# Conditioning pieces of the head: more places to load into, other moments for the loads, longer bursts

## The chip, the cores and the metric

The kernel runs on one core of a Trainium2 chip. The metric is the device time of one execution in microseconds. Three timed runs of the kernel before gave 1992.62, 1993.09 and 1994.77 us; their median is 1993.09 us. One more execution was profiled.

## The reference, cut to what matters

A decoder layer is run for 256 prompt tokens and 8 times 8 sample tokens (320 columns in all, width 2048). Only the first step matters here:

```python
mod = jax.nn.silu(c) @ w_ada + b_ada                      # (.., 6 * 2048), c: one row per sequence
sh1, sc1, g1, sh2, sc2, g2 = jnp.split(mod, 6, axis=-1)
h = _rmsnorm(x, norm1_g) * (1 + sc1) + sh1
p = h @ w_in                                              # 11280 columns
```

Before any row tile of h exists, its part of sh1 and sc1 must be there, which needs all 2048 rows of two column ranges of w_ada (2048 x 12288, float32). Everything after h (linear attention, pooling, w_o, the FFN) is the same in both kernels.

## The kernel before, in words

The part around the change is called the head. h is kept transposed, as 16 row tiles of 128 x 320, each split into a high and a low part (`hh`, `hl`). The 16 tiles are worked off in five slices, `SLICES` = 0-2, 2-4, 4-8, 8-12, 12-16. In each slice 15 units of 256 columns of w_in (the q, k, v, u, og, ga and gb columns of group 0, and the gb columns of groups 1 and 3) are multiplied by the tiles of that slice, and each unit's result is added in SBUF. A tile costs a unit two halves of three matmuls of 320 columns (lines 166 to 168), so a unit of a two-tile slice has 12 matmuls and a unit of a four-tile slice 24. In the two-tile slices the units v, og, ga and the three gb come in pairs that share one load (`proj_pair`); q, k and u are single.

While slice n is multiplied, `HeadJob` works out the conditioning (sh1, sc1) of the tiles of slice n+1: it loads w_ada in pieces of 512 KB (`load`), multiplies them on TensorE in bursts (`burst`, `ada_mm`, line 218; four column groups side by side, a float32 matmul shows as two instructions), then transposes the sums and adds the bias (`finish`), and `h_unit(k)` makes tile k of h from it. These steps stand in a list `bg`, and `after_unit` takes a share of them after each of the 15 units, so step i of a list of 15 runs after unit i. For a slice of two tiles there are four bursts, each of 32 instructions of 128 columns; for a slice of four tiles there are eight, each of 16 instructions of 256 columns.

Every load of w_ada and w_in is issued by one queue, SP's (line 142), and `keep_in_program_order` holds them there in the order in which the program calls them. A load waits on SP until its place in SBUF is free, and all loads behind it wait too. w_in has three places of 512 KB (`raw`), w_ada eight of 512 KB (`araw`). Each `burst` calls for the pieces of itself and of the next two bursts. When a piece of w_in has landed, ACT casts it to its high part (line 152), DVE makes the low part (line 153), and the matmuls start. Before the slices, x's rows stand in three tiles `xn0` to `xn2` of 128 x 2048; they are transposed into `xT` and then not read again; `junk`, of the same size, holds c's rows and the discarded squares. The slice-0 job has all eight `araw` places filled at the start. `spill` writes `xT` to DRAM through POOL's queue.

Of the kernel before, what the change touches and what calls it, by code (L numbers as in the profile page):

```python
# [11 lines left out]
F32 = mybir.dt.float32  # L12
# [8 lines left out]
P = 128  # L21
# [3 lines left out]
D = 2048  # L25
KT = D // P
# [12 lines left out]
SLICES = ((0, 2), (2, 4), (4, 8), (8, 12), (12, 16))  # L39
# [41 lines left out]
def body(tc, A):  # L81
# [15 lines left out]
    def nm(s):  # L97
        uid[0] += 1
        return "%s_%d" % (s, uid[0])

    def misc():
        return pmisc.tile([P, 512], F32, tag="m", name=nm("pm"))
# [32 lines left out]
    def raw_chunk(src, nk, nn, pool=None, tag="raw", bufs=3):  # L135

        if pool is None and more:
            more.reverse()
            if more[0] is not None:
                pool, bufs = more[0], 2  # L140
        t = (pool or wp).tile([P, nk, nn], F32, tag=tag, bufs=bufs, name=nm("raw"))
        ins = nc.sync.dma_start(t, src)
        if in_order[0]:
            tc.keep_in_program_order(ins)
        return t
# [63 lines left out]
    wada = A["w_ada"][0].rearrange("(kt p) n -> p kt n", p=P)  # L209
# [5 lines left out]
    def ada_mm(ps, k, raws, w, start=None, stop=None):  # L215

        for j in range(4):
            ins = PE.matmul(ps[32 * j:32 * j + 32, 0:w], lhsT=scT[:, k, :], rhs=raws[j],  # L218
                            start=k == 0 if start is None else start, stop=k == KT - 1 if stop is None else stop,
                            tile_position=(0, 32 * j))  # L220
            if j == 0:
                tc.keep_in_program_order(ins)

    def ada_out(dst, src, blk, shape):

        n = dst.shape[1]
        sec = blk // KT

        def wide(v):
            return v.rearrange("p (m c) -> p m c", m=shape[0]).unsqueeze(3).broadcast_to([P, *shape, 9])  # L230

        d4 = dst.rearrange("p (m c) r -> p m c r", m=shape[0])
        V.tensor_tensor(d4, src, wide(bada[:, blk:blk + n]), op=ALU.add)
        if sec in (1, 4):
            b0 = blk - sec * KT
            V.tensor_tensor(d4, d4, wide((N1G if sec == 1 else N2G)[:, b0:b0 + n]), op=ALU.mult)
# [53 lines left out]
    def modp(sec, kt):  # L290
        return mod[:, sec * KT + kt, 0:1]

    def mods(sec, kt):
        return mod[:, sec * KT + kt, 1:9].unsqueeze(2).broadcast_to([P, NB, LS])

    def s3(ap):
        return ap.rearrange("p (b t) -> p b t", t=LS)
# [79 lines left out]


    with tc.tile_pool(name="head", bufs=1) as xp:
        junk = xp.tile([P, D], F32, name="junk")  # L380
        crow = junk[0:9, :]
        nc.sync.dma_start(crow[0:1, :], A["c_prompt"])
        nc.sync.dma_start(crow[1:9, :], A["c_sample"])
        xn = [xp.tile([P, D], F32, name="xn%d" % i) for i in range(3)]
        x2d = A["x_prompt"][0]
        nc.sync.dma_start(xn[0], x2d[0:P])
        nc.sync.dma_start(xn[1], x2d[P:2 * P])
# [18 lines left out]
        def pinned(ins):  # L406
            tc.keep_in_program_order(ins)

        class HeadJob:


            def __init__(self, b0, s):
                self.b0, self.s, self.w, self.nk = b0, s, 64 * s, 8 // s
                self.ps = None
                self.raws = {}

            def load(self, k0):
                if k0 >= KT or k0 in self.raws:
                    return
                c = self.b0 * P  # L420
                self.raws[k0] = [raw_chunk(wada[:, k0:k0 + self.nk, sec * D + c:sec * D + c + self.s * P], self.nk,
                                  self.s * P, xp, "araw", 8) for sec in range(2)]

            def burst(self, k0):
                for ahead in range(3):
                    self.load(k0 + ahead * self.nk)
                raws = self.raws[k0]
                self.raws[k0] = None
                if self.ps is None:
                    self.ps = misc()  # L430
                w = self.w
                for i in range(self.nk):
                    ada_mm(self.ps, k0 + i, [raws[j // 2][:, i, (j % 2) * w:(j % 2) * w + w] for j in range(4)], w)

            def finish(self):
                nb = self.s // 2
# [6 lines left out]
                for sec in range(2):  # L443
                    blk = sec * KT + self.b0
                    ada_out(mod[:, blk:blk + self.s, :], src[:, 2 * sec:2 * sec + 2, :, 0:9], blk, (2, nb))

            def steps(self):
                return ([lambda: self.load(0)] + [lambda k0=k0: self.burst(k0) for k0 in range(0, KT, self.nk)]
                        + [self.finish])


        xT = []
        for k in range(KT):
            pt = misc()
            for i in range(3):
                n = P if i < 2 else TS
# [17 lines left out]
        for i in range(3):  # L474
            n = P if i < 2 else TS
# [5 lines left out]
        for i in range(3):  # L481
            n = P if i < 2 else TS
# [5 lines left out]
        def h_unit(k):  # L488
            t = xp.tile([P, T], F32, tag="xh", bufs=2, name=nm("xh"))
            V.scalar_tensor_tensor(t[:, 0:TP], xT[k][:, 0:TP], modp(1, k), rx[:, 0:TP], op0=ALU.mult, op1=ALU.mult)  # L490
            G.tensor_tensor(t[:, TP:T], xT[k][:, TP:T], rx[:, TP:T], op=ALU.mult)
            G.tensor_tensor(s3(t[:, TP:T]), s3(t[:, TP:T]), mods(1, k), op=ALU.mult)
            G.tensor_tensor(s3(t[:, TP:T]), s3(t[:, TP:T]), mods(0, k), op=ALU.add)
            S.activation(hh[k][:, 0:TP], t[:, 0:TP], AF.Identity, bias=modp(0, k))
            S.copy(hh[k][:, TP:T], t[:, TP:T])
            hl[k] = hp.tile([P, T], F32R, tag="hl%d" % k, name="hl%d" % k)
            V.scalar_tensor_tensor(hl[k][:, 0:TP], t[:, 0:TP], modp(0, k), hh[k][:, 0:TP].bitcast(F32),
                                   op0=ALU.add, op1=ALU.subtract)
            V.tensor_sub(hl[k][:, TP:T], t[:, TP:T], hh[k][:, TP:T].bitcast(F32))  # L499

        def spill(k0, k1):
            for k in range(k0, k1):
                pinned(nc.gpsimd.dma_start(xspill[k], xT[k]))
# [21 lines left out]
        for h in EARLY_GB:  # L525
            ge = G0()
            ge.gb = merged[h]
            early += [(ge, "gb", i, OGB + DV * h + 256 * i) for i in range(2)]
        for f in HeadJob(0, SLICES[0][1]).steps():
            f()  # L530
        for k in range(SLICES[0][1]):
            h_unit(k)
        for si, (k0, k1) in enumerate(SLICES):
            bg = []
            acc = 0 if si == 0 else 1
            if si + 1 < len(SLICES):
                n0, n1 = SLICES[si + 1]
                if si == 0:
                    bg.append(lambda: spill(0, SLICES[1][1]))
                else:  # L540
                    bg.append(lambda n0=n0, n1=n1: spill(n0, n1))
                bg += HeadJob(n0, n1 - n0).steps()
                bg += [lambda k=k: h_unit(k) for k in range(n0, n1)]
            if si == len(SLICES) - 2:
                walr = xp.tile([P, KT, 16], F32, name="walr")
                cum = xp.tile([P, NM0 + NM1 + NMS], F32, name="cum")

                def late_loads():
                    pinned(nc.gpsimd.dma_start(walr, win[:, :, OAL:OAL + 16]))
                    pinned(nc.gpsimd.dma_start(msk, A["ci"]))  # L550
                    pinned(nc.gpsimd.dma_start(cum, A["cf"][:, 64:CFW]))
                    pinned(nc.gpsimd.dma_start(invc, A["cf"][:, 0:64]))
                bg.insert(1, late_loads)
            def after_unit():
                count[1] += 1
                if si == len(SLICES) - 1 and count[1] == 2:
                    alr_proj(walr, cum)
                want = len(bg) * count[1] // len(early)
                while count[0] < want:
                    bg[count[0]]()  # L560
                    count[0] += 1

            count = [0, 0]
            e = 0
            while e < len(early):
                ge, kind, i, col = early[e]
                if k1 - k0 == 2 and kind not in "qku":
                    for half, ps in enumerate(proj_pair(win, col, k0, k1, hh, hl)):
                        evac(ps, ge, kind, half, acc)
                        after_unit()  # L570
                    e += 2
                else:
                    evac(proj(win, col, k0, k1, hh, hl), ge, kind, i, acc)
                    after_unit()
                    e += 1
# [436 lines left out]
    for ui in range(8):  # L1012
# [4 lines left out]
        for i in range(2):  # L1017
            residual(ps, i, 2 * ui + i, 2)
            k = 2 * ui + i
# [35 lines left out]
    for pi, (f0, f1) in enumerate(parts):  # L1055
# [22 lines left out]
        for ui in range(8):  # L1078
            ps = proj(wdn, 256 * ui, f0, f1, ah, al)
            for i in range(2):  # L1080
                k = 2 * ui + i
                residual(ps, i, k, 5)
                if pi == 1:
# [4 lines left out]
                    for a in range(3):  # L1088
                        n = P if a < 2 else TS
                        tr(pt[:n, a * P:(a + 1) * P], xg[:, a * P:a * P + n])  # L1090
                    for a in range(3):
                        n = P if a < 2 else TS
# [6 lines left out]
    for a in range(3):  # L1099
        n = P if a < 2 else TS  # L1100
        PE.matmul(pt[:n, 2 * a:2 * a + 2], lhsT=acc2[:, a * P:a * P + n], rhs=ones[:, 0:2], start=True, stop=True)
    rr = fp.tile([P, 64], F32, name="rr")[:, 0:6]
    for a in range(3):
        n = P if a < 2 else TS
# [3 lines left out]
    for a in range(3):  # L1108
        n = P if a < 2 else TS
# [30 lines left out]
```

## Time and profile before

| what | value |
|---|---|
| timed runs, median | 1993.09 us |
| profiled execution, its own time | 1993.81 us |
| span of the profile (first to last instruction) | 1992.0 us |
| PE busy | 1942.7 us, 98% |
| DVE, ACT, POOL busy | 51%, 41%, 7% |
| DMA, mean over the span | 201 GB/s |
| granted TensorE clock, mean | 0.991 |

The profiled execution's time is its span and 1.8 us around it. A busy share of an engine is that of the time in which an instruction of it was running. DMA share is the busy share of the core's 16 DMA engines; it can read a little above 1 where packets overlap.

### The profile page before, as it was taken

The numbers are of one execution on the slowest core, as the hardware profiler recorded it, in microseconds if no ns is written. First come the engines' busy times: TensorE is split into PE (matmuls) and PEld (weight loads), VectorE is DVE, ScalarE is ACT, GpSimd is POOL, SyncE is SP. The second block draws the span as 40 slices with busy tenths as digits, with TensorE's granted clock in tenths as the row PEclk, the third lists the DMA queues.
The fourth block names the chain that finished last, engine by engine and source line by source line (L and its number), as shares of the span: only waits on it lengthen the run. The fifth ranks groups of instructions, "written<-read, shape, count | busy, mean of one in ns | idle before, by whom it ended". The sixth has DMA issues, their size and how long they took to land.

```text
span 1992.0 us, 37175 instructions
## 1 busy us (share of the span) xinstructions
PE 1942.7 (98%) x15008; PEld 1848.6 (93%) x15008; DVE 1014.1 (51%) x1881; ACT 819.6 (41%) x1468; POOL 137.5 (7%) x261
## 2 busy tenths in 40 slices
PE   7999999999999999999989999999999999999997
PEld 5789998898999899889979999999999999999997
DVE  2556665574546544664574444344444444444554
ACT  4333374364335333643353333343333434344443
POOL 1112220111011100110030000000000000000000
PEclk9999999999999999999989999999999999999998
DMA  9888754775975787579636666544445544444442
GB/s 296 287 303 271 230 165 147 263 262 187 325 245 174 269 266 234 167 248 339 226 112 223 202 221 193 167 150 143 156 147 151 153 152 148 149 148 149 148 143 90
DMA packets 319598, 400.83 MB, mean 201 GB/s; under 512 B 13529, under 2 KB 259801, under 8 KB 319089
## 3 DMA queue, kind: packets, MB, share of 16 engines
q1 hardware_dynamic: 307154, 358.21, 56.1%
q0 software_dynamic: 12272, 40.25, 5.4%
q8 instruction: 117, 1.92, 0.4%
q14 instruction: 55, 0.45, 0.1%
HBM read 373.96 MB, written 24.67 MB: 200 GB/s over the span
## 4 chain that ended last, share of the span: by engine, by line
PE 93%; DMA 4%; DVE 1%; ACT 1%; issue 1%; SPq 0%; POOL 0%; ACTq 0%; POOLq 0%; DVEq 0%
PE ps L166 27%; PE ps L168 27%; PE ps L167 27%; PE pm L218 5%; PE pm L129 2%; DMA raw<-w_ada 1%; DMA raw<-w_in 1%; DMA raw<-w_o 1%; PE pm L804 1%; PE pm L825 1%; PE pm L773 1%; DMA xn<-x_sample 1%; PE pm L800 0%; PE pm L762 0%; DVE wlo L153 0%
## 5 line engine op out<-in xcount | busy, mean ns | idle before, releaser
L153 DVE TENSOR_TENSOR wlo<-raw,whi 128x512 fp32r<-128x512 f32 x952 | 658.6, 696 | 817.5 <-ACT whi L152 807.5
L152 ACT CAST whi<-raw 128x512 fp32r<-128x512 f32 x952 | 586.3, 621 | 995.4 <-PE ps L167 843.8
L166 PE MATMUL ps<-hh,whi 128*128 128x320 f32 x1408 | 443.3, 315 | 6.5 <-ACT whi L152 3.0
L166 PE MATMUL ps<-h2h,whi 128*128 128x320 f32 x1408 | 437.4, 311 | 5.1 <-ACT h2h L1046 5.1
L168 PE MATMUL ps<-hh,wlo 128*128 128x320 f32 x1408 | 440.4, 313 | 0.1
L167 PE MATMUL ps<-hl,whi 128*128 128x320 f32 x1408 | 438.7, 312 | 0.4 <-DVE hl L499 0.4
L168 PE MATMUL ps<-h2h,wlo 128*128 128x320 f32 x1408 | 435.5, 309 | 0.0
L167 PE MATMUL ps<-h2l,whi 128*128 128x320 f32 x1408 | 435.5, 309 | 0.0
L166 PEld LDWEIGHTS ps<-hh,whi 128*128 128x128 f32 x1408 | 265.6, 189 | 25.6 <-issue 11.8
L168 PEld LDWEIGHTS ps<-hh,wlo 128*128 128x128 f32 x1408 | 265.6, 189 | 7.9 <-issue 5.7
L166 PEld LDWEIGHTS ps<-h2h,whi 128*128 128x128 f32 x1408 | 265.0, 188 | 8.5 <-ACT h2h L1046 6.1
L167 PEld LDWEIGHTS ps<-hl,whi 128*128 128x128 f32 x1408 | 265.7, 189 | 7.5 <-issue 5.9
L167 PEld LDWEIGHTS ps<-h2l,whi 128*128 128x128 f32 x1408 | 264.9, 188 | 0.0
L168 PEld LDWEIGHTS ps<-h2h,wlo 128*128 128x128 f32 x1408 | 264.9, 188 | 0.0
L166 PE MATMUL ps<-ah,whi 128*128 128x320 f32 x704 | 218.7, 311 | 0.0
L168 PE MATMUL ps<-ah,wlo 128*128 128x320 f32 x704 | 217.5, 309 | 0.0
L167 PE MATMUL ps<-al,whi 128*128 128x320 f32 x704 | 217.5, 309 | 0.0
L167 PEld LDWEIGHTS ps<-al,whi 128*128 128x128 f32 x704 | 132.2, 188 | 0.0
L166 PEld LDWEIGHTS ps<-ah,whi 128*128 128x128 f32 x704 | 132.2, 188 | 0.0
L168 PEld LDWEIGHTS ps<-ah,wlo 128*128 128x128 f32 x704 | 132.2, 188 | 0.0
L218 PE MATMUL pm<-raw,scT 128*32 128x128 f32 (+1 forms) x2688 | 104.7, 296 | 4.3 <-DMA raw<-w_ada 4.3
L218 PEld LDWEIGHTS pm<-raw,scT 128*32 128x32 f32 x2688 | 72.0, 112 | 25.3 <-issue 13.6
(279 smaller groups left out, 1538.2 us busy)
## 6 DMA issues: line engine op xcount, KB each, us to landing
raw<-w_ada SPq DMA_DIRECT2D x192, 512.0 KB, 6.1
raw<-w_gu SPq DMA_DIRECT2D x176, 512.0 KB, 3.5
raw<-w_in SPq DMA_DIRECT2D x173, 512.0 KB, 4.3
raw<-w_down SPq DMA_DIRECT2D x80, 512.0 KB, 3.4
S<-state_gla POOLq DMA_DIRECT2D x16, 1024.0 KB, 8.7
o_gs<-S POOLq DMA_DIRECT2D x16, 1024.0 KB, 7.6
raw<-w_o SPq DMA_DIRECT2D x32, 512.0 KB, 5.3
raw<-w_down SPq DMA_DIRECT2D x16, 256.0 KB, 2.5
```

Of the source, the lines that this page charges most:

```text
L129: PE.transpose(out, in_, ident[:k, :k])
L152: S.copy(hi, raw)
L153: V.tensor_sub(lo, raw, hi.bitcast(F32))
L166: PE.matmul(ps, lhsT=whi, rhs=xhi, start=start, stop=False)
L167: PE.matmul(ps, lhsT=whi, rhs=xlo, start=False, stop=False)
L168: PE.matmul(ps, lhsT=wlo, rhs=xhi, start=False, stop=stop)
L218: ins = PE.matmul(ps[32 * j:32 * j + 32, 0:w], lhsT=scT[:, k, :], rhs=raws[j], start=k == 0 if start is None else start, stop=k == KT - 1 ...
L773: PE.matmul(pt, lhsT=E["kdn"][:, s, d * P:(d + 1) * P], rhs=E["vn"][:, s], start=s == 0, stop=s == 1)
L804: PE.matmul(pt[32 * j:32 * j + 32, :], lhsT=qeP[:, d, 4 * gg + j, :], rhs=E["S0", gg, d][:, j], start=False, stop=d == 1, tile_position=(0 ...
L825: PE.matmul(pt, lhsT=kpz[:, gg, j, d * P:(d + 1) * P], rhs=E["vp"][:, gg], start=True, stop=True)
```

## The change

Three things change in `HeadJob` and in the lists that call it.

- w_ada pieces get four more places of 1 MB each: the tiles `xn0`, `xn1`, `xn2` and `junk`, once x's rows are done with. Pieces of 1 MB go there, pieces of 512 KB to `araw` as before.
- The bursts are longer. The slice of two tiles behind slice 0 has two bursts of eight row tiles (64 instructions of 128 columns); a slice of four tiles has four bursts of four row tiles (32 instructions of 256 columns). Slice 0's own job keeps four bursts of 32 instructions.
- The loads are steps of their own. In slice 0 all 4 MB of slice 1's job are called for after units 1 and 2, and the four bursts' pieces of slice 2's job (2 MB each) after units 8, 11, 14 and 15. In slice 1 and 2 the pieces of the job two slices on follow after units 5, 8, 12 and 15. Bursts come after units 7 and 10 in slice 0, and after units 2, 4, 7 and 9 later (in the fourth slice one step list is longer by one).

```diff
@@ class HeadJob
-            def load(self, k0):
-                if k0 >= KT or k0 in self.raws:
-                    return
+                if b0 == 0:
+                    self.bursts = [[(k, 4)] for k in range(0, KT, 4)]
+                elif s == 2:
+                    self.bursts = [[(0, 8)], [(8, 8)]]
+                else:
+                    self.bursts = [[(0, 2), (2, 2)], [(4, 2), (6, 2)], [(8, 4)], [(12, 4)]]
+            def load(self, b):
                 c = self.b0 * P
-                self.raws[k0] = [raw_chunk(wada[:, k0:k0 + self.nk, sec * D + c:sec * D + c + self.s * P], self.nk,
-                                  self.s * P, xp, "araw", 8) for sec in range(2)]
+                for k, n in self.bursts[b]:
+                    for sec in range(2):
+                        src = wada[:, k:k + n, sec * D + c:sec * D + c + self.s * P]
+                        if n * self.s == 8:
+                            r = raw_chunk(src, n, self.s * P, xp, "araw", 8)
+                        else:
+                            r = raw_chunk(src, n, self.s * P, xp, BIG[2 * (b % 2) + sec], 1)
+                        self.raws[k, sec] = r
-            def burst(self, k0):
-                for ahead in range(3):
-                    self.load(k0 + ahead * self.nk)
...
+            def burst(self, b):
...
+                todo = [(k, i) for k, n in reversed(self.bursts[b]) for i in range(n)]
+                for k, i in todo:
+                    ada_mm(self.ps, k + i, ...)
...
@@ the lists
-        for f in HeadJob(0, SLICES[0][1]).steps():
-            f()
+        jobs = [HeadJob(k0, k1 - k0) for k0, k1 in SLICES]
+        for b in range(4):
+            jobs[0].load(b)
+        for b in range(4):
+            jobs[0].burst(b)
+        jobs[0].finish()
...
                 if si == 0:
-                    bg.append(lambda: spill(0, SLICES[1][1]))
+                    bg += [load(job, 0), load(job, 1), sp, rest, rest, rest, burst(0), load(nxt, 0), rest, burst(1),
+                           load(nxt, 1), job.finish, hu[0], load(nxt, 2), hu[1], load(nxt, 3)]
                 else:
-                    bg.append(lambda n0=n0, n1=n1: spill(n0, n1))
-                bg += HeadJob(n0, n1 - n0).steps()
-                bg += [lambda k=k: h_unit(k) for k in range(n0, n1)]
+                    bg += [sp, burst(0), rest, burst(1), load(nxt, 0), rest, burst(2), load(nxt, 1), burst(3),
+                           job.finish, hu[0], load(nxt, 2), *hu[1:], load(nxt, 3)]
```

`BIG` is ("xn0", "xn1", "xn2", "junk"), `job` the job of the next slice, `nxt` that of the slice after it, `rest` an empty step, `sp` the spill, `hu` the h_units.

## Rows read from the trace of the kernel before

**Rows 1.** Stretches of 25 us: length, busy of each engine, clock, DMA share, GB/s

```profile
25.00:50.00 25.00, 21.29 (x243) 19.07 (x243) 9.22 (x24) 8.72 (x18) 5.57 (x11) 0.93 0.87 293
...
75.00:100.00 25.00, 21.95 (x204) 16.27 (x196) 12.24 (x20) 6.42 (x11) 0.00 (x0) 1.00 0.89 315
...
150.00:175.00 25.00, 25.00 (x190) 23.72 (x180) 18.59 (x36) 10.77 (x22) 10.09 (x20) 1.00 0.66 198
```

**Rows 2.** Timeline of PE in slice 1: start, duration, instruction, idle before and releaser

```profile
83.17 0.41 PE L166 MATMUL ps<-hh,whi 128*128 128x320 f32 x1 [1.41 <-ACT whi L152]
...
90.92 0.41 PE L166 MATMUL ps<-hh,whi 128*128 128x320 f32 x1 [1.63 <-ACT whi L152]
...
109.84 0.39 PE L166 MATMUL ps<-hh,whi 128*128 128x320 f32 x1 [0.33 <-DVE hl L499]
```

**Rows 3.** Timeline of SP's queue, ahead of the first of these waits

```profile
75.87 0.88 SPq L142 DMA_DIRECT2D raw<-w_ada  x2
76.85 0.42 SPq L142 DMA_DIRECT2D raw<-w_in  x1
```

**Rows 4.** Timeline of PE around three bursts, of 32, 16 and 48 instructions

```profile
51.30 0.31 PE L167 MATMUL ps<-hl,whi 128*128 128x320 f32 x1
51.45 0.31 PE L168 MATMUL ps<-hh,wlo 128*128 128x320 f32 x1
51.69 1.08 PE L218 MATMUL pm<-raw,scT 128*32 128x128 f32 x32
52.70 0.41 PE L166 MATMUL ps<-hh,whi 128*128 128x320 f32 x1
52.95 0.31 PE L167 MATMUL ps<-hl,whi 128*128 128x320 f32 x1
...
125.79 1.07 PE L218 MATMUL pm<-raw,scT 128*32 128x256 f32 x16
...
315.31 1.52 PE L218 MATMUL pm<-raw,scT 128*32 128x128 f32 x48
316.76 0.40 PE L644 MATMUL pm<-cumr,w 128*128 128x272 f32 x1
```

**Rows 5.** Instructions by line on PE, 35.00 to 69.39 us (slice 0)

```profile
L166 PE MATMUL ps<-hh,whi 128*128 128x320 f32 x60 | 19.6, 329 | 2.9 <-ACT hh L495 2.7 <-DVE v L355 0.2
```

**Rows 6.** Timeline of PE: the last transposes of x's rows

```profile
23.17 1.63 PE L129 MATMUL pm<-cst,xn 128*128 128x128 f32 x5
```

**Rows 7.** Stretches in which the DMA engines were full, columns as in rows 1

```profile
14.00:24.00 10.00, 10.00 (x34) 5.06 (x34) 3.37 (x11) 5.08 (x11) 0.00 (x0) 1.00 1.10 349
...
29.50:45.50 16.00, 12.46 (x131) 11.21 (x124) 6.43 (x18) 5.34 (x11) 5.25 (x10) 0.89 1.00 330
...
79.00:94.00 15.00, 11.95 (x104) 9.20 (x103) 5.80 (x10) 2.28 (x4) 0.00 (x0) 1.00 1.02 373
...
99.00:119.00 20.00, 19.45 (x137) 17.84 (x137) 16.65 (x33) 8.60 (x18) 7.46 (x16) 1.00 1.01 365
```

**Rows 8.** DMA issues of the first 300 us: count, size, median us to landing

```profile
raw<-w_ada SPq DMA_DIRECT2D x67, 512.0 KB, 6.4
```

**Rows 9.** The loads of w_ada and w_in as one tile, first 300 us

```profile
DMA to landing us min/median/max: 2.8/5.8/13.1
```

**Rows 10.** Timeline of ACT: a cast that waited for its load

```profile
90.25 1.14 ACT L152 CAST whi<-raw 128x512 fp32r<-128x512 f32 x2 [6.61 <-DMA raw<-w_in]
```

**Rows 11.** Timeline of PE at the start of slice 0

```profile
35.33 0.56 PE L166 MATMUL ps<-hh,whi 128*128 128x320 f32 x2 [2.67 <-ACT hh L495]
...
38.58 0.47 PE L166 MATMUL ps<-hh,whi 128*128 128x320 f32 x1
38.85 0.47 PE L167 MATMUL ps<-hl,whi 128*128 128x320 f32 x1
```

**Rows 12.** A stretch inside it, columns as in rows 1

```profile
38.00:39.40 1.40, 1.40 (x7) 1.40 (x7) 0.00 (x0) 0.00 (x0) 0.65 (x2) 0.50 1.03 312
```

**Rows 13.** GB/s of the first 300 us in 40 equal slices

```profile
GB/s 242 281 348 206 307 365 286 185 260 360 346 344 317 261 399 335 188 302 327 242 210 107 225 337 393 320 316 336 205 192 143 140 325 377 193 142 95 101 141 114
```

More of the change, by code (lines that the diff above doesn't have):

```diff
@@ L379, in body @@
     with tc.tile_pool(name="head", bufs=1) as xp:
-        junk = xp.tile([P, D], F32, name="junk")
+        BIG = ("xn0", "xn1", "xn2", "junk")
+        junk = xp.tile([P, D], F32, tag="junk", name="junk")
         crow = junk[0:9, :]
@@ L383, in body @@
         nc.sync.dma_start(crow[1:9, :], A["c_sample"])
-        xn = [xp.tile([P, D], F32, name="xn%d" % i) for i in range(3)]
+        xn = [xp.tile([P, D], F32, tag="xn%d" % i, name="xn%d" % i) for i in range(3)]
         x2d = A["x_prompt"][0]
@@ L412, in __init__ @@
             def __init__(self, b0, s):
-                self.b0, self.s, self.w, self.nk = b0, s, 64 * s, 8 // s
+                self.b0, self.s, self.w = b0, s, 64 * s
                 self.ps = None
                 self.raws = {}
-            def load(self, k0):
-                if k0 >= KT or k0 in self.raws:
-                    return
-                c = self.b0 * P
-                self.raws[k0] = [raw_chunk(wada[:, k0:k0 + self.nk, sec * D + c:sec * D + c + self.s * P], self.nk,
-                                  self.s * P, xp, "araw", 8) for sec in range(2)]
-            def burst(self, k0):
-                for ahead in range(3):
-                    self.load(k0 + ahead * self.nk)
-                raws = self.raws[k0]
-                self.raws[k0] = None
+                if b0 == 0:
[5 more added lines that the diff above has]
+            def load(self, b):
+                c = self.b0 * P
+                for k, n in self.bursts[b]:
[7 more added lines that the diff above has]
+            def burst(self, b):
                 if self.ps is None:
@@ L431, in burst @@
                 w = self.w
-                for i in range(self.nk):
-                    ada_mm(self.ps, k0 + i, [raws[j // 2][:, i, (j % 2) * w:(j % 2) * w + w] for j in range(4)], w)
+                todo = [(k, i) for k, n in reversed(self.bursts[b]) for i in range(n)]
+                for k, i in todo:
+                    ada_mm(self.ps, k + i,
+                           [self.raws[k, j // 2][:, i, (j % 2) * w:(j % 2) * w + w] for j in range(4)], w,
+                           b == 0 and (k, i) == todo[0], b == len(self.bursts) - 1 and (k, i) == todo[-1])
             def finish(self):
@@ L445, in finish @@
                     ada_out(mod[:, blk:blk + self.s, :], src[:, 2 * sec:2 * sec + 2, :, 0:9], blk, (2, nb))
-            def steps(self):
-                return ([lambda: self.load(0)] + [lambda k0=k0: self.burst(k0) for k0 in range(0, KT, self.nk)]
-                        + [self.finish])
         xT = []
@@ L537, in body, with load, burst, rest @@
                 n0, n1 = SLICES[si + 1]
+                job = jobs[si + 1]
+                nxt = jobs[si + 2] if si + 2 < len(SLICES) else None
+                def load(j, b):
+                    return (lambda: j.load(b)) if j else (lambda: None)
+                def burst(b):
+                    return lambda: job.burst(b)
+                def rest():
+                    return None
+                hu = [lambda k=k: h_unit(k) for k in range(n0, n1)]
+                sp = lambda n0=n0 if si else 0, n1=n1: spill(n0, n1)
                 if si == 0:
-                    bg.append(lambda: spill(0, SLICES[1][1]))
-                else:
-                    bg.append(lambda n0=n0, n1=n1: spill(n0, n1))
-                bg += HeadJob(n0, n1 - n0).steps()
-                bg += [lambda k=k: h_unit(k) for k in range(n0, n1)]
+                    bg += [load(job, 0), load(job, 1), sp, rest, rest, rest, burst(0), load(nxt, 0), rest, burst(1),
+                           load(nxt, 1), job.finish, hu[0], load(nxt, 2), hu[1], load(nxt, 3)]
+                else:
+                    bg += [sp, burst(0), rest, burst(1), load(nxt, 0), rest, burst(2), load(nxt, 1), burst(3),
+                           job.finish, hu[0], load(nxt, 2), *hu[1:], load(nxt, 3)]
             if si == len(SLICES) - 2:
```

## Prediction

> **What bounds the kernel now.** Over the whole span PE is busy 98% of the time, so a change can win only where PE idles or where it does needless work. I read first the stretches of 25 us, because the change touches only the head (about the first 240 us). There PE is short of work twice: 3.7 us between 25 and 50, and 3.0 us between 75 and 100; by 150 to 175 it has no idle time while DMA is at two thirds [rows 1]. Second, the timeline of PE says what ended those gaps. The first is the wait for the first tile of h, before slice 0, which the change leaves alone. The second is two waits in slice 1, 1.41 and 1.63 us, both ended by ACT's cast of a w_in piece [rows 2]. Third, SP's queue says why that cast was late: the w_in load went out at 76.85, directly behind two w_ada pieces that had waited at 75.87 for a burst to free their places [rows 3]. So PE bounds the head from slice 2 on, and in slices 0 and 1 it runs close to what the DMA queue delivers: DMA is 0.87 to 0.89 busy there [rows 1].
>
> **The bursts.** Matmuls of the main stream start 0.147 us apart (51.30 to 51.45 shows 0.15). Around a burst of 32 instructions the starts run 51.45, 51.69, 52.70, 52.95: 1.50 us where two steps would be 0.29, so the burst costs 1.21 us. A burst of 48 runs 1.45 us from its start to the next matmul against 1.01, so 16 more instructions of 128 columns cost 0.44, and of the 1.21 us some 0.33 are entry and exit. Sixteen instructions of 256 columns take 1.07 against 1.08, the same [rows 4]. A burst of the new size is 64 instructions of 128 columns or as much: 1.21 + 2 x 0.44 = 2.09 us. The job run in slice 0 had four bursts (4.84) and gets two (4.18): 0.66 saved. Each of the three four-tile jobs had eight (9.68, or 9.6 with the 256-column rows) and gets four (8.36): 1.2 saved each. Together 4.3 us, all on PE and so on the path. No row shows a burst of this length: it can't cost more than two of 32 (2.42, nothing saved), nor less than its instructions without any entry (1.76, some 9 saved over the 14 bursts); the step from 32 to 48 is the nearest row, so I take 2.09. The two waits of slice 1 are worth 3.0 more if nothing replaces them.
>
> **The loads.** Here I add up what SP's queue must move in program order. A w_ada piece is 512 KB, 0.524 MB [rows 8]; a 1 MB piece is two of them. A single unit of a two-tile slice loads 0.262 MB, a pair 0.524. Ahead of the first w_in load of slice 1 now stand all of slice 1's job (8 x 0.524 = 4.19 MB), all of slice 2's job (8.39 MB; before only slice 1's job stood there), slice 0's w_in (3.93 MB), four spills of 0.164 MB on the other queue (0.66), and the load itself (0.26): 17.4 MB.
>
> When does this start? The first two pieces go into xn0 and xn1, whose last transposes end at 23.17 + 1.63 = 24.8 [rows 6]. The quickest landing of all was 2.8 us, for a load whose bytes take some 0.8 of it, so about 2.0 us are fixed [rows 9]; the queue flows from 26.8. How fast? Stretches with the engines full gave 349 and 330 GB/s early on, where the loads are 256 columns wide, and 373 and 365 later, where most are 512 wide [rows 7]. I take 340 and 370, near the middle of each pair. 5.24 MB are of the narrow kind (slice 1's job, q, k, u, and q again): 15.4 us. 12.19 MB of the wide kind: 32.9 us. The load of slice 1's q lands at 26.8 + 48.3 = 75.1. From cast start to matmul is 0.7 us (90.25 to 90.92) [rows 10, 2], so PE starts slice 1 at 75.8.
>
> PE would be ready sooner. Slice 0 is 180 matmuls (60 by each of three lines) and ends at 69.4 before [rows 5]; less 0.66 that is 68.7. So PE waits 7.1 us where it now waits for nothing. Two smaller things inside slice 0 are covered: the v pair, now behind 4.2 MB, lands at 26.8 + 5.0 / 0.34 = 41.4, within 1 us of need, and that slip is swallowed by the 7.1.
>
> Such a wait has a second price. After 2.67 us idle PE came back at the lower level: starts 0.27 us apart, granted clock 0.50, that is 1.2 GHz and not 2.4, for 4 us, some 1.9 us lost; after the waits of 1.41 and 1.63 the clock was 1.00 [rows 11, 12, 2, 1].
>
> Slice 1 then goes so. q and k take 24 x 0.147 + 1.9 = 5.4 us, the first burst 2.1: 83.3. Only then are the places free for the next four 512 KB pieces, which SP holds ahead of og's load; the queue has run dry by then. og lands at 83.3 + 2.0 + 2.62 / 0.37 = 92.4 and starts at 93.1, where PE (v, a burst, u: 7.4 us) was ready at 90.7: 2.4 us of waiting, in place of the 3.0 that go away. PE then needs 17.7 us for the five pairs and 4.2 for two bursts: 114.9 or so. The queue has to bring four pairs (2.10 MB), the pieces of three more bursts (6.29), the spills (0.66) and slice 2's first load (0.52), 9.57 MB, 25.9 us: 118.3, start of slice 2 at 119.0. Before, it started at 109.84 [rows 2].
>
> From there on PE has enough in hand (DMA at 0.66, [rows 1]); slices 2 and 3 give back their 1.2 each. Sum: 9.2 - 2.4 = +6.8 us. On the profiled execution's 1993.8 (span 1992.0 and 1.8 around it) that is 2000.6; it stood 0.7 above the median of the runs, so I predict 2000.
>
> In this sum the step that hurts is not a slower instruction but the order: bytes that slices 2 and 3 have time for are put in front of bytes that slices 1 and 2 need at once. Finish and h_units come at the same units or one earlier, so they cost nothing: DVE, ACT and POOL have half their time free there [rows 1].
>
> **What the queue can deliver decides.** The same sum with one rate for all: at 340 GB/s slice 2 starts at 124.8, +12.6 us; at 379, a bit above the best stretch, 115.9, +3.6; at 405 the first wait is 1.8 us, no clock falls, and it is 108.9, -3.3; from 410 on it is -4.2 or better. The best 7.5 us slice moved 399 [rows 13], but with less in its neighbours. If the clock falls again at the start of slice 2, 1.9 more; if it doesn't fall at all, 1.9 less.
>
> The Trainium skill speaks for both sides. Its HBM Reference, section Specifications (TRN2), gives a core about 358 GB/s effective, and well above that, about 425, when it streams alone, as here. By the first the sum would be an estimated +8, by the second -6.4, a result of its own. The full stretches of this trace (365 to 373) lie near the first.
>
> **Rivals.** *The queue is fuller than any stretch shows, and the waits go* (faster): with four more places SP is seldom blocked, and loads 512 wide and longer in a row could run above the 373. It decides at 410 GB/s, where the sum reaches -4.2; with every wait gone the gain is 4.3 + 3.0 = 7.3, at best 1986. For it: the 399 slice. Against it: four stretches with a DMA share of 1.00 or more and 330 to 373 [rows 7]. Chance 0.14, at 1986 to 1989. The 425 GB/s of the Trainium skill's HBM Reference would make it an estimated 1986.7.
>
> *A draw*: the queue runs at 380 to 405, or PE's clock stays up through the waits; the new waits are as long as the savings, +3.6 to -3.3. This is also the case that the change does nothing that can be measured, since the pieces are prefetched but the same bytes bound the same slices. Chance 0.28, at 1990 to 1997.
>
> *The forecast*: 340 to 372 GB/s, waits at the starts of slices 1 and 2. Its own range is 1997 to 2004, chance 0.52.
>
> *Heavy*: everything near 340, since 1 KB rows and spills share the queue, or the clock falls at each of three waits: +9 to +14. Chance 0.06.
>
> **How the numbers follow.** A measurement of this kernel tells apart about 0.2%, 4 us: the bounds are 1989.1 and 1997.1. Faster 0.14, same 0.28, slower 0.58. The range of 8 in 10 leaves out most of the first rival and the far end of the last: 1990 to 2008 reaches from a queue at 405 to one at 330 to 340.
>
> **What would show it.** In the profile after: 14 bursts of the new size, near 1.9 us from start to next matmul, beside slice 0's own four (32 bursts before); the DMA share at 1.0 from 27 to 75 us; PE's first matmul of slice 1 near 75 with some 5 to 7 us idle before it and a half clock after it; a gap in the queue around 80 to 85 while SP waits for a burst; slice 2 starting after 114. Wrong would be: slice 1 starting by 70, which means a queue above 410 or loads that went out earlier than xn's release; or w_in loads that pass the w_ada pieces on SP.

## The result, and the profile after

The changed kernel takes 2001.55 us (median of 6 runs, 1998.59 to 2007.23), against 1993.09 before: a ratio of 1.0049, 95% interval 1.0035 to 1.0063. By the medians it is slower by 8.5 us, where 6.9 were predicted. Two slow runs (2714.78 us in experiment 2, and 2366.35 us of the kernel before, run beside experiments 9 and 10) are left out of all medians and ratios below. The profiled execution has a span of 1999.2 us (1992.0 before) and a mean granted clock of 0.988 (0.991).

The stretches of 25 us, with the columns of [rows 1], and below the "..." others that the text comes back to:

```profile
25.00:50.00 25.00, 18.46 (x188) 15.41 (x186) 8.35 (x22) 7.32 (x15) 4.80 (x11) 0.86 0.88 293
50.00:75.00 25.00, 23.72 (x253) 22.94 (x254) 11.80 (x24) 10.14 (x20) 3.07 (x8) 0.93 1.05 390
75.00:100.00 25.00, 20.01 (x159) 16.94 (x157) 11.13 (x18) 5.62 (x10) 1.20 (x3) 0.93 0.86 312
100.00:125.00 25.00, 22.74 (x178) 19.45 (x177) 18.62 (x36) 9.62 (x21) 7.11 (x16) 0.95 0.86 307
150.00:175.00 25.00, 25.00 (x209) 22.75 (x208) 15.47 (x30) 10.16 (x22) 5.55 (x13) 1.00 0.82 290
27.00:75.00 48.00, 40.19 (x433) 36.84 (x433) 20.03 (x45) 16.42 (x33) 7.86 (x19) 0.89 0.98 351
45.00:50.00 5.00, 3.70 (x24) 3.31 (x23) 2.87 (x5) 1.90 (x4) 0.00 (x0) 1.00 0.57 174
50.00:55.00 5.00, 3.72 (x16) 3.73 (x17) 2.02 (x3) 2.08 (x4) 0.00 (x0) 0.66 1.05 398
80.00:85.00 5.00, 4.92 (x54) 3.76 (x53) 2.88 (x5) 1.66 (x3) 0.00 (x0) 1.00 0.23 69
...
36.50:43.40 6.90, 5.60 (x22) 4.65 (x20) 0.98 (x3) 1.24 (x3) 2.25 (x5) 0.55 1.07 383
50.20:53.60 3.40, 2.32 (x9) 2.33 (x10) 2.02 (x3) 1.53 (x3) 0.00 (x0) 0.59 1.06 402
...
94.90:98.40 3.50, 3.46 (x13) 3.46 (x14) 2.57 (x4) 1.65 (x3) 0.00 (x0) 0.54 1.05 390
...
121.90:125.30 3.40, 3.27 (x13) 3.27 (x14) 2.64 (x6) 1.19 (x3) 0.00 (x0) 0.58 0.67 220
```

PE is short of 6.5 us between 25 and 50 (3.7 before) and of 5.0 between 75 and 100 (3.0 before), and from 50 to 75 the DMA share has risen from 0.79 to 1.05. That stretch in the kernel before:

```profile
50.00:75.00 25.00, 25.00 (x245) 23.55 (x248) 15.65 (x29) 11.49 (x22) 5.11 (x10) 1.00 0.79 262
```

The PE timeline says which waits these are; each line starts after the idle time in its bracket:

```profile
39.72 0.63 PE L166 MATMUL ps<-hh,whi 128*128 128x320 f32 x1 [1.30 <-ACT whi L152]
44.78 0.42 PE L166 MATMUL ps<-hh,whi 128*128 128x320 f32 x1 [1.30 <-ACT whi L152]
51.28 0.64 PE L166 MATMUL ps<-hh,whi 128*128 128x320 f32 x1 [2.57 <-ACT v L353]
...
77.89 0.41 PE L166 MATMUL ps<-hh,whi 128*128 128x320 f32 x1 [1.42 <-ACT whi L152]
...
94.94 0.46 PE L166 MATMUL ps<-hh,whi 128*128 128x320 f32 x1 [3.08 <-ACT whi L152]
...
120.44 0.41 PE L166 MATMUL ps<-hh,whi 128*128 128x320 f32 x1 [0.60 <-ACT whi L152]
...
122.03 0.41 PE L168 MATMUL ps<-hh,wlo 128*128 128x320 f32 x1 [1.03 <-DVE wlo L153]
```

The first three lie inside slice 0; 77.89 is the start of slice 1, 94.94 is og's first matmul, 120.44 is the start of slice 2 (109.84 in [rows 2]). SP's queue shows why slice 1 is late; a duration that is long for its count is time in which the queue was held:

```profile
31.19 15.26 SPq L142 DMA_DIRECT2D raw<-w_in  x4
46.54 2.12 SPq L142 DMA_DIRECT2D raw<-w_ada  x4
...
60.04 8.36 SPq L142 DMA_DIRECT2D raw<-w_ada  x4
68.50 10.46 SPq L142 DMA_DIRECT2D raw<-w_in  x4
...
83.38 1.90 SPq L142 DMA_DIRECT2D raw<-w_ada  x4
```

q's load for slice 1, the first at 68.50, goes out behind four 1 MB pieces, whose last pair had to wait for the burst that begins at 65.42 and ends at 67.3. It lands at 77.2. The group at 83.38 is the wait foreseen in slice 1: the burst at 82.28 frees its places only then, and between 80 and 85 the queue moves 69 GB/s.

The bursts themselves do what they were costed at. PE around one of 64 instructions, and one of 32 instructions of 256 columns:

```profile
57.82 0.31 PE L168 MATMUL ps<-hh,wlo 128*128 128x320 f32 x1
58.06 1.95 PE L218 MATMUL pm<-raw,scT 128*32 128x128 f32 x64
59.94 0.41 PE L166 MATMUL ps<-hh,whi 128*128 128x320 f32 x1
60.20 0.31 PE L167 MATMUL ps<-hl,whi 128*128 128x320 f32 x1
...
87.97 1.93 PE L218 MATMUL pm<-raw,scT 128*32 128x256 f32 x32
89.84 0.41 PE L166 MATMUL ps<-hh,whi 128*128 128x320 f32 x1
```

From 57.82 to 60.20 are 2.38 us where two steps would be 0.29: the burst costs 2.09, as estimated from [rows 4].

To compare executions I use a mark at the head's end, the first matmul of the small projection that follows the second unit of the last slice. Before (first fence) and after (second fence), timeline of PE:

```profile
243.26 0.31 PE L516 MATMUL pm<-hh,wal 128*64 128x320 f32 x1
```

```profile
252.94 0.31 PE L526 MATMUL pm<-hh,wal 128*64 128x320 f32 x1
```

Counted from slice 0's first matmul (35.33 and 35.77) the head has grown from 207.9 to 217.2 us, by 9.2. Slice 0 with the wait behind it takes 8.0 more (42.1 against 34.1), slice 1 2.1 more (42.6 against 40.4), slices 2 and 3 up to the mark 0.9 less. Behind the mark the profiled execution of before lost 2.5 us more than that of after, so the spans differ by 7.2 only; there it has, among others, a wait of 2.53 us for a w_ada piece at 691.91 that after does not have.

A part of the 9.2 us is the clock. In the four stretches from 25 to 125 us, what the granted clock lacks to 1.00 adds up to 8.3 us in after and 1.8 in before. That is an upper bound for its price, since PE also waits inside some of this time.

### The profile page after: what moved, and what is told of

The parts are those of the page before. It is cut to its first block, busy times and chain, and to the rows that moved or that the text cites. A ratio compares the mean times of both kernels' runs of the same rounds, so it can differ in the third digit from the quotient of the medians.

```text
span 1999.2 us, 37162 instructions
## 1 busy us (share of the span) xinstructions
PE 1943.1 (97%) x15008; PEld 1854.1 (93%) x15008; DVE 1015.4 (51%) x1881; ACT 820.1 (41%) x1468; POOL 135.3 (7%) x261
## 4 chain that ended last, share of the span: by engine, by line
PE 92%; DMA 4%; DVE 1%; ACT 1%; issue 1%; POOL 0%; SPq 0%; ACTq 0%; DVEq 0%; POOLq 0%
PE ps L166 27%; PE ps L167 27%; PE ps L168 27%; PE pm L218 4%; DMA raw<-w_ada 2%; PE pm L129 2%; DMA raw<-w_in 1%; PE pm L832 1%; PE pm L853 1%; PE pm L801 1%; DMA xn<-x_prompt 1%; DVE wlo L153 0%; DMA raw<-w_o 0%; PE pm L828 0%; PE pm L790 0%
## 5 line engine op out<-in xcount | busy, mean ns | idle before, releaser
L218 PE MATMUL pm<-raw,scT 128*32 128x128 f32 (+1 forms) x2688 | 100.7, 293 | 3.1 <-DMA raw<-w_ada 2.9
```

## The experiments

Three theories were put to the test. **A**: the bytes that the queue has to bring ahead of w_in's loads set when slices 1 and 2 start. **B**: what costs is inside slice 0: ACT's order there (q's evacuation, the copy of its finished sums into SBUF, at 38.46 stands ahead of k's cast at 39.06, k's at 43.52 ahead of v's cast) and the clock around those waits. **C**: the longer bursts or the 1 MB pieces are slow in themselves. Except for one, each kernel is the changed one with the edit shown. "Head" is the time from slice 0's first matmul to the mark, of the profiled execution; the timed ratio is to the kernel before, on the same chip. ACT's order in after, on which B rests:

```profile
38.46 0.70 ACT L353 ACTIVATE q<-ps 128x640 f32<-128x640 f32 x1 [1.93 <-PE ps L168]
39.06 0.61 ACT L152 CAST whi<-raw 128x512 fp32r<-128x512 f32 x1
43.52 0.70 ACT L353 ACTIVATE k<-ps 128x640 f32<-128x640 f32 x1 [3.85 <-PE ps L168]
44.12 1.65 ACT L152 CAST whi<-raw 128x512 fp32r<-128x512 f32 x3
```

| kernel | head, us | timed median, us | ratio to before, 95% interval |
|---|---|---|---|
| before | 207.9 | 1993.09 | |
| after | 217.2 | 2001.55 | 1.0049 (1.0035 to 1.0063) |
| 1 late halves | 214.2 | 1996.45 | 1.0016 (1.0007 to 1.0025) |
| 2 just in time | 214.4 | 1992.96 | 1.0002 (0.9993 to 1.0011) |
| 3 w_in first | 213.5 | 1995.33 | 1.0013 (1.0005 to 1.0022) |
| 4 half the bytes | 205.9 | 1988.44 | 0.9978 (0.9969 to 0.9987) |
| 5 all moved | 213.1 | 1995.14 | 1.0018 (1.0010 to 1.0027) |
| 6 split halves | 206.5 | 1989.51 | 0.9987 (0.9978 to 0.9996) |
| 7 short bursts on 5 | 211.1 | 1993.72 | 1.0016 (1.0007 to 1.0025) |
| 8 k's cast first | 218.4 | 2001.72 | 1.0052 (1.0039 to 1.0065) |
| 9 long bursts alone | 236.1 | 2018.27 | 1.0133 (1.0117 to 1.0148) |
| 10 short bursts on 6 | 212.2 | 1994.65 | 1.0013 (1.0004 to 1.0022) |

The two columns do not always agree. By the heads, experiments 1 to 3 win back a third of the 9.2 us (3.0, 2.8 and 3.7), by the ratios two thirds to all of the loss. The head is from one execution, and the program behind the mark, the same in all kernels, took anything from 1743.1 us (experiment 1) to 1749.0 us (experiment 7) in the twelve profiled ones. So whether a kernel is faster is read from the ratios, and the profiles serve to read which wait went where; what part of a ratio each wait is worth stays open to a few us.

**1. Late halves.** The third and fourth load of each four-tile job move into the slice in which they are multiplied.

```diff
-  load(nxt, 1), job.finish, hu[0], load(nxt, 2), hu[1], load(nxt, 3)]
+  load(nxt, 1), job.finish, hu[0], rest, hu[1], rest]
-  bg += [sp, burst(0), rest, burst(1), load(nxt, 0), rest, burst(2), ...
+  bg += [sp, burst(0), load(job, 2), burst(1), load(nxt, 0), load(job, 3), burst(2), ...
```

> Theory A (bytes put in front of w_in on SP's queue set the starts of slices 1 and 2): with the second half of each four-tile job (4.2 MB) called for one slice later, the load of slice 1's q lands some 11 us sooner than the 77.2 of the changed kernel, slice 1 then starts where slice 0 ends (76.3 with the waits that slice 0 has of its own), og in slice 1 still waits about 3 us because its load stands behind pieces that wait for a burst, and slice 2 starts near 116 instead of 120.4: about 1996 us, some 5 below the changed kernel. Theory B (the casts of slice 0 stand behind evacuations in ACT's order, and the clock falls in those waits): slice 0 is untouched, so 2001, within 1.5 us. Theory C (pieces of 1 MB or bursts twice as long are slow in themselves): 2001.

Slice 1 now begins at 74.15 without a wait, and by the ratio the kernel wins back two thirds of the loss, as A forecast. The waits inside slice 0 stay (1.30, 1.30, 2.29), and some remain in slice 1 (2.56 at 89.78, 1.71 at 109.75). Slice 2 begins at 117.63, later than the 116 expected.

**2. Just in time.** As 1, with the loads of the next job at units 8 and 12 and not 5 and 8.

```diff
-  bg += [sp, burst(0), load(job, 2), burst(1), load(nxt, 0), load(job, 3), burst(2), load(nxt, 1), burst(3),
+  bg += [sp, burst(0), load(job, 2), burst(1), load(job, 3), rest, burst(2), load(nxt, 0), burst(3),
-         job.finish, hu[0], rest, *hu[1:], rest]
+         job.finish, hu[0], load(nxt, 1), *hu[1:], rest]
```

> As the run before, and in slices 1 and 2 the first half of the next job is called for three to four units later, when the burst that frees its places is long done. Theory A: the 3.1 us wait before og and its stretch at half clock go too, slice 2 starts near 111: 1990 to 1992 us. Theory B: 2000 to 2001, since slice 0's waits stay. Theory C: 2001.

The whole loss is gone (1.0002), though the time is a little above the 1990 to 1992 us expected. Orders of the same loads, with the same bursts and places, thus span some 9 us. That speaks for A and against C. The profiled execution does not show the path that A foresaw, though: its head is like that of 1, PE still waits 2.14 us at 89.11, and slice 2 begins at 117.84 after a wait of 2.30 us, not near 111. The queue is full from 75 to 100:

```profile
75.00:100.00 25.00, 22.69 (x197) 18.80 (x196) 10.11 (x16) 5.21 (x9) 0.00 (x0) 0.93 1.04 388
```

**3. w_in first.** Only slice 1's job is called for three units later (behind the loads of v and u instead of q and k); what stands ahead of slice 1's first load is the same.

```diff
-  bg += [load(job, 0), load(job, 1), sp, rest, rest, rest, burst(0), ...
+  bg += [rest, rest, sp, load(job, 0), load(job, 1), rest, burst(0), ...
```

> The changed kernel with slice 1's job called for behind the loads of v and u instead of behind those of q and k; the sum of bytes ahead of slice 1's first load is the same 17.4 MB. Theory A: the waits inside slice 0 (1.3, 1.3 and 2.6 us) go, but slice 1 still starts at 76 to 78, when its first load lands: 2000 to 2002 us, no change. Theory B: slice 0 ends at 69 to 70 and the head is some 7 us shorter: 1994.

The time is near B's 1994, and A as I had put it, no change, is refuted. But slice 0 does not end at 69 to 70, as B said: it ends at 73.8, just when slice 1's first load lands. The trace of this kernel, its stretch from 45 to 50, ACT's cast of slice 1's first piece, and PE's start on it:

```profile
45.00:50.00 5.00, 3.81 (x25) 3.40 (x24) 2.85 (x6) 2.67 (x5) 0.00 (x0) 1.00 1.05 399
```

```profile
73.74 0.62 ACT L152 CAST whi<-raw 128x512 fp32r<-128x512 f32 x1 [0.99 <-DMA raw<-w_in]
```

```profile
74.41 0.42 PE L166 MATMUL ps<-hh,whi 128*128 128x320 f32 x1 [0.65 <-ACT whi L152]
```

The hole of after at 45 to 50 (174 GB/s) is not there (399). By the stretches of 5 us from 25 to 70 this kernel's queue moved 16.36 MB, after's 15.13: 1.23 MB more, 3.2 us at 390 GB/s. Slice 1 begins 3.3 us sooner after the start of slice 0 (38.8 against 42.1 us). So A needs a word more: it is the bytes and the holes. After's hole begins while SP holds four w_in loads for 15.26 us, which fits places that are freed by casts that come late.

**4. Half the bytes.** The four-tile jobs load one of their two column ranges and use it for both; the other half (4.2 MB of each job) is left out.

```diff
+  if sec == 1 and self.s == 4:
+      self.raws[k, 1] = self.raws[k, 0]
+      continue
```

> The changed kernel, but the jobs of the three four-tile slices load the columns of one of their two sections only and use them for both, so 4.2 MB of each 8.4 MB are left out and the output is not the reference's; places, bursts and the moments of the loads are unchanged. Theory A: slice 1's q lands some 11 us sooner, slice 1 starts where slice 0 ends, the wait before og is short, slice 2 starts at 109 to 112: 1989 to 1993 us. Theory B: 1999 to 2001, only slice 0's last wait can shrink. Theory C: 2001, since the bursts and the places are the same.

With the bursts and steps untouched the kernel is 4.4 us faster than before (by the ratio), 13 us faster than after. It leaves little for C. That the bursts were to save just as much (4.3 us, to 1988.8) is in part chance: the head is only 2.0 us shorter than before, and PE's waits of more than 0.45 us in it still add up to 6.7 us (3.0 before). The edit also leaves out half of the loads and of the places that they hold, so it does not part the bytes from the waiting for places.

**5. All moved.** The slice 0 list of 3 without its last two loads, with the list of 2 for the later slices.

> Slice 1's job called for behind v and u, as in the run that did this alone, and the second halves and next jobs called for later, as in the just-in-time run. Theory A with its correction (bytes in front of w_in, and holes in the queue while SP waits for a w_in place whose cast is late): both waits go, slice 0 ends near 70, slice 1 has one wait of at most 2 us, the alr projection starts near 243 where the just-in-time run had 248.9: 1986 to 1990 us, below the kernel before. Theory B alone (order of ACT in slice 0) would give the gain of the w_in-first run and no more on top of it: 1993 to 1995.

A miss by 5 us, and the time is that of 3, as B alone forecast. The two moves don't add up. The profile gives a reason other than B: slice 0 ends at 73.1 and not near 70, and the queue now idles where it could have worked and is crowded afterwards, as two stretches of this kernel show:

```profile
75.00:100.00 25.00, 22.49 (x196) 18.54 (x200) 11.73 (x18) 5.28 (x9) 0.00 (x0) 0.93 1.05 398
...
60.00:70.00 10.00, 9.12 (x107) 7.66 (x106) 6.20 (x14) 5.45 (x13) 4.81 (x9) 1.00 0.27 70
```

PE waits 1.74 us at 88.93 and 2.62 at 116.76. What was too much ahead of slice 1 in after is too little here; 6 tests that.

**6. Split halves.** As 5, but one more load (2 MB) goes into that hole, and one is left for the next slice.

```diff
-  load(nxt, 1), job.finish, hu[0], rest, hu[1], rest]
+  load(nxt, 1), job.finish, hu[0], load(nxt, 2), hu[1], rest]
-  bg += [sp, burst(0), load(job, 2), burst(1), load(job, 3), rest, burst(2), load(nxt, 0), burst(3),
-         job.finish, hu[0], load(nxt, 1), *hu[1:], rest]
+  bg += [sp, burst(0), load(job, 3), burst(1), rest, rest, burst(2), load(nxt, 0), burst(3),
+         job.finish, hu[0], load(nxt, 1), *hu[1:], load(nxt, 2)]
```

> As the run before, but the third burst's pieces of each four-tile job are again called for at the end of the slice before (2.1 MB, where the queue has a hole otherwise) and only the fourth's in the slice itself. Corrected theory A: 15.3 MB ahead of slice 1's first load land by 67 to 69, in time, and the wait in slice 1 shrinks: 1985 to 1989 us, 0 to 2 below the run before. If what counts is only that fewer bytes stand ahead of slice 1, it is 2 to 4 slower than the run before.

This is faster than both kernels, 5.6 us below 5 where 0 to 2 were expected, and 0.5 above the range. The same two stretches, and PE's largest wait behind slice 0:

```profile
75.00:100.00 25.00, 24.84 (x238) 19.94 (x239) 15.10 (x25) 6.66 (x12) 0.00 (x0) 1.00 1.05 400
...
60.00:70.00 10.00, 9.33 (x109) 8.03 (x108) 5.20 (x13) 4.72 (x11) 3.49 (x7) 1.00 0.66 235
```

```profile
111.90 0.41 PE L166 MATMUL ps<-hh,whi 128*128 128x320 f32 x1 [0.81 <-ACT whi L152]
```

The clock is 1.00 in all stretches from 50 to 125; PE is busy for 24.84 of the 25 us from 75 to 100 (21.95 in [rows 1], 20.01 in after). With bursts and places as in after, this rules out C as the cause of the loss. Not all is won: slice 0 takes 37.8 us from its first matmul to slice 1's, where it took 34.1 before; slice 1 takes 2.5 less than before, and slices 2 and 3 up to the mark 2.7 less.

**7 and 10. Short bursts.** On 5 and on 6, each of the 14 long bursts is run as two halves, after neighbouring units; the loads stay at their steps. On 5 some added halves run a unit earlier than the long burst did and some a unit later; on 6 all second halves run a unit later, so that places come free later too.

```diff
-  for k, i in todo:
+  m = len(todo) // 2
+  for k, i in (todo if part is None else todo[part * m:(part + 1) * m]):
```

> The run with everything moved, each long burst split into two halves that run after two neighbouring units; loads and bytes are the same. If a burst's entry and exit cost 0.33 us of PE, 14 more of them in the head cost 4.6: 4 to 5 us above the run with everything moved. If the matmuls around a burst cover its entry, or if the wait for pieces sets the pace anyway, within 1.5 us of it.

> The version of the run before the last but one that beat both kernels (loads of slice 2's and 3's jobs split between two slices), with each of its 14 long bursts run as two of half the length after neighbouring units; loads at the same steps. There PE has no wait over 0.81 us behind the first units, so PE's own work sets the pace: 14 more entries into a burst at 0.3 to 0.33 us are 4.2 to 4.6 us more, 1993.5 to 1994.5 against 1989.5. The rival: loads still set the pace, as where the same edit was made with all loads moved and cost nothing; then within 1.5 us of 1989.5.

On 6 it costs 5.1 us of the median, 5.7 of the head: near the 4.2 to 4.6 expected, though with it come a wait that grew from 0.81 to 1.60 us and a clock of 0.93 from 100 to 125 us (1.00 in 6). On 5 it costs nothing; the waits of 1.74 and 2.62 us are gone (behind slice 0 one of 1.24 us is left), so PE spends on entries what it spent on waiting. That fits an entry price of 0.3 us, which counts only where PE sets the pace; how much of the 5.1 us is the later freeing of places was not separated.

**8. k's cast first.** In slice 0 ACT's order is pinned so that k's cast runs ahead of q's evacuation (line numbers of this kernel are 1 to 3 higher).

```diff
...
+  held = split_chunk(win[:, k0:k1, early[1][3]:early[1][3] + 256], 2, 256)
+  pin_act[0] = True
+  held = list(held)
+  evac(psq, ge, kind, i, acc)
+  pin_act[0] = False
...
```

> The changed kernel with one swap in ACT's order: the cast of k's piece in slice 0 ahead of q's evacuation, with all loads, bytes and bursts as they are. Corrected theory A with B in it: the 1.3 us wait at k goes, k's place comes free some 3 us sooner, so og's load goes out sooner and the hole in the queue between 40 and 50 us shrinks; slice 1 starts 2 to 3 us sooner: 1998 to 1999 us. Theory A as first stated (bytes alone): 2001, no change.

PE's and SP's timelines of this kernel:

```profile
43.06 0.41 PE L169 MATMUL ps<-hh,whi 128*128 128x320 f32 x1 [3.46 <-ACT whi L153]
49.44 0.41 PE L169 MATMUL ps<-hh,whi 128*128 128x320 f32 x1 [2.46 <-ACT v L356]
...
77.44 0.63 PE L169 MATMUL ps<-hh,whi 128*128 128x320 f32 x1 [4.12 <-ACT whi L153]
```

```profile
56.89 8.28 SPq L143 DMA_DIRECT2D raw<-w_ada  x4
65.27 13.25 SPq L143 DMA_DIRECT2D raw<-w_in  x4
```

The time, 2001.72, is not the 1998 to 1999 forecast but that of A as first stated. k's wait is gone (v's is longer, but in this execution the clock stays at 1.00), and slice 0's work is done some 3 us sooner (its bursts at 54.91 and 62.27, not 58.06 and 65.42). q's load goes out 3.2 us sooner too, but lands at 76.8, only 0.4 sooner: the 11.5 us from 65.27 to 76.8 are 4.5 MB at 390 GB/s, which are the four 1 MB pieces ahead of q (4.19) and q itself (0.26). The time won in slice 0 turns into a wait of 4.12 us at slice 1. B falls, as far as this swap tests it: slice 0 still has two long waits, but it ends at 73.3, before the load that slice 1 needs lands at 76.8.

**9. Long bursts alone.** The kernel before, with its eight places and its order of loads, where two neighbouring bursts run as one in the later one's step.

```diff
+  if self.b0 and k0 // self.nk % 2 == 0:
+      return
-  raws = self.raws[k0]
...
+  for k1 in ([k0 - self.nk, k0] if self.b0 else [k0]):
+      raws = self.raws[k1]
...
```

> The kernel before with one part of the change alone: two neighbouring bursts are run as one, in the later one's step, from slice 1's job on; places, loads and their order stay those of the kernel before. 14 entries into a burst at 0.3 to 0.33 us go away. If PE's own work sets the pace of all five slices, 4.3 us less: about 1988 to 1989.5. The rival: in slices 1 and 2 the loads set the pace, and the earlier piece of each pair keeps its place one unit longer, so that SP holds the loads behind it; then only the bursts of slices 2 and 3 pay (2.4 us), the waits of slice 1 (1.41 and 1.63 us before) grow, and it is 1990 to 1993, within 0.2% of before. A third: the long bursts themselves cost more than 2.1 us each; then no gain at all, 1992.5 or more.

Far worse than any theory said: 26.0 us over before's median on that chip. The mechanism is the rival's, its price was mis-sized. SP's and PE's timelines of this kernel in slice 1:

```profile
78.78 13.82 SPq L142 DMA_DIRECT2D raw<-w_ada  x4
92.70 0.41 SPq L142 DMA_DIRECT2D raw<-w_in  x1
```

```profile
84.93 0.64 PE L166 MATMUL ps<-hh,whi 128*128 128x320 f32 x1 [4.38 <-ACT whi L152]
90.25 1.93 PE L218 MATMUL pm<-raw,scT 128*32 128x256 f32 x32
100.29 0.64 PE L166 MATMUL ps<-hh,whi 128*128 128x320 f32 x1 [7.33 <-ACT whi L152]
```

SP stands at pieces whose places the burst at 90.25 frees, w_in's load comes behind them at 92.70, and PE waits 7.33 us for it. The same happens in every later slice (2.59 at 143.95, 2.76 at 157.93, 2.71 at 219.53, 2.63 at 233.15). So in the old order of loads the long bursts cost far more than they save; the change's parts can't be priced one by one, and places without long bursts were not run.

## Why the prediction was right, and where its terms were off

Slower, by bytes in front of w_in's loads: that was the forecast, and it held. Experiments 1, 2 and 6 took two thirds of the loss or more back by order alone, experiment 4 by leaving out bytes (and the places they hold), and in experiment 8 time won elsewhere in slice 0 was no help. That the figure is so close, 2000 against 2001.55, is partly luck: several terms were off and offset each other. The terms:

- **The bursts**: 2.09 us as estimated, read directly in the profile of after. The 4.3 saved in all follow from it and from the cost of the short bursts; experiment 10, which pays back 5.1, fits them without showing them alone.
- **q's load at 75.1, slice 1 at 75.8**: 77.2 and 77.89. The byte sum was right: 351 GB/s from 27 to 75 is 16.8 MB, and some 0.7 more until 77.2 make 17.5, where 17.4 was counted. Two errors in the rate offset each other, by luck. The full queue is faster than I took it (390 to 398 GB/s against 370), but I had it full throughout, and it had a hole at 45 to 50 that costs 1.1 MB, 2.9 us.
- **The wait of 7.1 us at slice 1, and "two smaller things inside slice 0 are covered"**: the place was wrong. Only 1.42 us are left at slice 1, since slice 0 itself ends at 76.3 and not 68.7: three waits of 1.30, 1.30 and 2.57 us, and a granted clock of 0.55 from 36.5 to 43.4 and of 0.59 from 50.2 to 53.6. I had put v's slip at 1 us, and had not looked at what stands on ACT ahead of a cast that is late. The sum is nearly the same because these losses lie under the wait for q (experiment 8).
- **One fall of the clock, 1.9 us**: there were three more than before that count, behind 51.28, 94.94 and 122.03, and the one at the start of slice 0 lasted longer; one at the start of slice 2 was named as a possible 1.9 us. The clock's part is up to 6.5 us more than in before, where 1.9 were counted. The fall foreseen behind slice 1's start didn't come; the wait there was 1.42 us and not 7.1.
- **og at 93.1 after 2.4 us**: 94.94 after 3.08, behind the burst at 82.28 as foreseen (83.3).
- **Slice 2 at 119.0**: 120.44. **2.4 us given back by slices 2 and 3**: 0.9 up to the mark; the 1.03 us wait for wlo and the 3.4 us near half clock around it take more than the difference.

Together 9.2 us of the head where 6.8 were expected. Of the rivals, the faster one needed a queue above 410 GB/s: it was full at 390 to 400. Had it never run dry, the prediction's sums (+3.6 at 379, -3.3 at 405) give +0.7 to -2 at 390 to 400, the draw; the holes decided against that. Experiment 6, which fills a part of the hole at 60 to 70 that 5 has (235 GB/s against 70), shows that a part of the bursts' gain can be had: 2.6 us by the ratio (0.8 to 4.4). Of the two figures of the Trainium skill's HBM Reference (Specifications (TRN2)), 358 and 425 GB/s, the full stretches lie about halfway between, and the mean with holes (351) lies near the first.

Not settled: how the loss divides between bytes, held places and holes in the queue; why slice 0 stays 3.7 us or more longer than before in every version of the changed kernel; why ACT's order in slice 0 is what it is, and which of its casts opened the hole at 45 to 50. Experiment 3 removed hole and late casts together, and experiment 8 made it shallower (269 and 313 GB/s from 40 to 50) and yet moved slice 1's start by 0.4 us only.

## What to carry to other kernels

When loads of two kinds share one queue in program order, count the bytes and the occupied places ahead of each load that is needed soon: a prefetch that is early enough for its user can still be too early for the load behind it. More places and longer bursts paid only once each load stood late enough not to delay w_in and early enough to leave no hole in the queue; both errors cost 5 to 10 us here, and the cure for one brought on the other (experiment 5). And price a saving on the engine where that engine sets the pace: the same added burst entries cost some 5 us in one order of loads and nothing in another.

## What was not expected of the hardware

- A full queue of 1 and 2 KB rows moved 388 to 400 GB/s for 25 us at a time (50 to 75 in after, 75 to 100 in experiments 2, 5 and 6), where the best full stretch of [rows 7] was 373 over 15 us.
- The length of a wait alone does not tell whether TensorE comes back at 1.2 GHz. In after, waits of 0.60 and 1.03 us close together at 120.44 and 122.03 were followed by a granted clock of 0.58, and in before waits of 1.41 and 1.63 by 1.00; in experiment 8, waits of 2.23, 3.46 and 2.46 us in slice 0 left it at 1.00 from 25 to 75.
- Behind the head the clock falls at places that differ between executions. The same instructions follow the same wait (1.38 us at 280.52 in before, 1.37 at 290.20 in after), once with a fall of the clock and once without. Before (first fence) and after (second fence), each around this wait:

```profile
278.00:284.00 6.00, 4.62 (x22) 3.96 (x21) 5.79 (x8) 5.94 (x12) 1.31 (x1) 0.82 0.34 93
```

```profile
287.70:293.70 6.00, 4.63 (x28) 3.96 (x27) 5.80 (x8) 5.94 (x12) 1.30 (x1) 1.00 0.33 92
```

With a spread of 5.9 us behind the mark in the twelve profiles, one span against another says little about differences of a few us, and the timed runs decide on those.
